# A retention and conformer trunk on one core: the conv module in one written order, scores a head ahead, heads turned amid pooled rows

## The chip, the cores and the metric

The kernel runs on one core of a Trainium2 chip. The metric is the device time of one execution in microseconds (us), as the median of several runs. TensorE (PE) multiplies 128x128 blocks; VectorE (DVE), ScalarE (ACT) and GpSimd (POOL) work on 128-partition tiles in SBUF and PSUM; SyncE (SP) issues the transfers.

## What is computed

512 tokens of width 1024 pass four pre-normalised residual layers: a mixer, a SwiGLU feed-forward layer (FFN), a convolution module, and a second FFN; then a final norm.

```
# mixer: retention (4 heads of 128) beside a pooling mixer
q, k, v, g, u = split(h @ w_in)
scores = einsum('bhncd,bhnmd->bhncm', qc, kc) * decay_mask
o      = scores @ v + cross-chunk state;  o = groupnorm(o) * ret_norm_g
out    = concat([silu(g) * o, pooled(u)]) @ w_out
# conformer conv
a, gate = split(h @ w_pw1 + b_pw1)
u  = a * sigmoid(gate)
dw = depthwise_conv(u, w_dw, width 31, causal) + b_dw
z  = silu(layernorm(dw) * ln_g + ln_b)          # over channels
out = z @ w_pw2 + b_pw2
```

## The kernel before

**Numbers.** Each f32 operand is split into a high part (fp32r) and a low rest, and a product is three matmuls: high by high, low by high, high by low (`mm3`, L224 to L226). Activations lie with channels on the partitions and 512 tokens along the row, eight tiles of 128 channels. Weights come as 1-MB chunks: a transfer (L167), a cast of the high part on ACT (L195), a subtraction for the low part on DVE (L198). PE runs its instructions in the order in which they stand; so do the other engines. PSUM holds three pairs of banks for products ("mm") and two single banks ("aux").

**The mixer.** q and k of a head are split (`parts`), a head's scores are four blocks of products (`ps_s`) that DVE multiplies by the decay mask into `sT` (L516), and the outputs `ps_o` are products of `sT` and v (L520). Head h's scores stand right ahead of its outputs. The out-projection (`ps_wo`) sums over eight rows of blocks, the four pooled ones first; when it reaches a retention head, that head is turned by four transposes (`ps_t`, L563), scaled and split (`mh`, L252), and used at once.

**The conv module.** The first projection runs in eight chunks `ps_pw j` of 48 products with 512 columns; `gated` turns a chunk into u_j (DVE L1085, sigmoid on ACT, DVE L1088). Tiles 0 and 1 are convolved on DVE, 31 multiply-adds each ("taps", L1114). Tiles 2 to 7 are convolved on PE (`ps_c`, L1122): 32 matmuls on 32-row quadrants, of shifted copies R_j of u_j (four transfers inside SBUF, L1103) by diagonal blocks dg_j that POOL multiplies (L1097; two buffers, so dg_j waits for conv tile j-2). The layer norm's sums are taken about a pivot: the mean over channels of tiles 2 and 3, added on DVE (`pivot`, L1183), summed over partitions by PE (`ps_ms`, L304), scaled (L1185), spread to all partitions by PE (`ps_mu`, L312). From then on DVE keeps sums of d and of its square.

For j below 6 the code is a loop, and the instructions of each engine are ordered by a scheduler. From chunk 6 on the order is written out by hand: chunks 6 and 7 and the conv tiles 6 and 7 go in two halves A and B of 256 tokens, and for each half come the sums, `stats`, then `centre`, `swish` (L1167, L1171, L1173) and `split_z` (high part on DVE, L1177; rest, L1178), and the second projection `ps_p` (L245 to L248).

Of the kernel before, what the change touches and what calls it, by code (L numbers as in the profile page):

```python
# [9 lines left out]
F32 = mybir.dt.float32  # L10
# [6 lines left out]
P = 128  # L17
D = 1024
S = 512
# [63 lines left out]
def trunk(ctx: ExitStack, tc: tile.TileContext, a: dict):  # L83
# [54 lines left out]
    halved = {("w_pw1", 6), ("w_pw1", 7), ("w_pw2", 0), ("w_pw2", 1)}  # L138
# [4 lines left out]
    def start_load():  # L143
# [18 lines left out]
        elif i == 1:  # L162
            raw = raws[1]
            for s in CUT[1][1:]:
                nc.sync.dma_start(raw[:, s], a[name][j][:, s])
        else:
            nc.sync.dma_start(raw[:, :kt * c], a[name][j])  # L167
# [69 lines left out]
    def high_first(ps, wh, wl, xh, xl, cols, ks):  # L237

        for low in range(2):
            for k in ks:  # L240
                for i in range(2):
                    c = slice(i * P, (i + 1) * P)
                    o = ps[:, i, cols]
                    if low:
                        nc.tensor.matmul(o, lhsT=wh[:, k, c], rhs=xl[k][:, cols], start=False, stop=k == KT - 1)  # L245
                    else:
                        nc.tensor.matmul(o, lhsT=wh[:, k, c], rhs=xh[k][:, cols], start=k == 0, stop=False)
                        nc.tensor.matmul(o, lhsT=wl[:, k, c], rhs=xh[k][:, cols], start=False, stop=False)  # L248
# [102 lines left out]
    def mixer():  # L351
        nonlocal xin
        with ExitStack() as m:
# [128 lines left out]
            v = [xp.tile([P, S], F32, tag=f"xgl{t}", name=f"v{t}") for t in range(NT)]  # L482
            token_major("v", lambda t, ps: nc.vector.tensor_scalar_mul(v[t], ps, rtok[:, t:t + 1]))


            def parts(h):
                odd = h % 2
                out = []
                for i, src in enumerate((qk[h], qk[4 + h])):
                    if odd:  # L490
# [6 lines left out]
                    out.append((h_, l_))  # L497
                return out


            pos_ = [pair(f"ps_o{i}") for i in range(2)]
            ahead = parts(0)
            for h in range(H):
                (qh, ql), (kh, kl) = ahead
                ahead = parts(h + 1) if h + 1 < H else None
                sT = []
                for j in range(NT):
# [9 lines left out]
                    sT.append(s)  # L517
                for i in range(NT):
# [33 lines left out]
            acc = new_acc()  # L552
            for j2 in range(2):
                ws = [chunk("w_o", 2 * j2 + jj) for jj in range(2)]
                pss = [pair(f"ps_wo{2 * j2 + jj}") for jj in range(2)]
                for ks in ((4, 5, 6, 7), (0, 1, 2, 3)):
                    for jj in range(2):
                        wh, wl = ws[jj]
                        for k in ks:
                            if mh[k] is None:  # L560
                                pt = paux.tile([P, S], F32, tag="aux", name=f"ps_t{k}")
                                for t in range(NT):
                                    nc.tensor.transpose(pt[:, t * P:(t + 1) * P], ret[t][:, k * P:(k + 1) * P], ident)  # L563
                                mh[k] = mx.tile([P, S], F32R, tag=f"xgh{k}", name=f"mh{k}")
                                ml[k] = mx.tile([P, S], F32R, tag=f"xgl{k}", name=f"ml{k}")
                                split_scaled(mh[k], ml[k], pt, V("ret_g", k))
# [496 lines left out]
    def conv(acc):  # L1063
        with ExitStack() as m:
# [10 lines left out]
            us, Rs, dgs = {}, {}, {}  # L1075

            def gated(j, ps, cols, between=lambda: None):
# [12 lines left out]
                if j < NDVE:  # L1090
                    return

                if j not in Rs:
                    Rs[j] = cw.tile([P, 4, 28 + S], F32, tag="R", name=f"R{j}")
# [11 lines left out]
            def conv_tile(j, cols, between={}):  # L1106
                if j < NDVE:
                    o = d[:, j, cols]
                    for q in range(CW):
                        at = slice(1 + q + cols.start, 1 + q + cols.stop)  # L1110
                        if q == 0:
                            nc.vector.tensor_scalar(o, us[j][:, at], V("dwc", CW * j), V("b_dw", j), ALU.mult, ALU.add)
                        else:
                            nc.vector.scalar_tensor_tensor(o, us[j][:, at], V("dwc", CW * j + q), o, ALU.mult, ALU.add)  # L1114
                else:
                    ps = paux.tile([P, S], F32, tag="aux", name=f"ps_c{j}")
                    n = cols.stop - cols.start
                    for g in range(8):
                        if g in between:
                            between[g]()  # L1120
                        for i in range(4):
                            nc.tensor.matmul(ps[32 * i:32 * i + 32, :n], lhsT=dgs[j][:, i, g, :],  # L1122
                                             rhs=Rs[j][:, i, 4 * g + cols.start:4 * g + cols.stop],
                                             start=g == 0, stop=g == 7, skip_group_check=True)
                    return ps[:, :n]
# [11 lines left out]
            def second_sums(j, cols):  # L1137
                sq = s2 if j == PV[0] else wk.tile([P, cols.stop - cols.start], F32, tag="sq", name="sqc")
                nc.scalar.activation(sq, d[:, j, cols], AF.Square)
                if j != PV[0]:  # L1140
                    nc.vector.tensor_tensor(s2[:, cols], s2[:, cols], sq, ALU.add)

            def pivot_tile(j, ps, cols):
# [4 lines left out]
                second_sums(j, cols)  # L1148
# [26 lines left out]
            def split_z(j, cols):  # L1175
                dj = d[:, j:j + 2, cols]
                nc.vector.tensor_copy(zh[:, j:j + 2, cols], dj)  # L1177
                nc.vector.tensor_tensor(zl[:, j:j + 2, cols], dj, zh[:, j:j + 2, cols].bitcast(F32), ALU.subtract)  # L1178
# [3 lines left out]
            def pivot():  # L1182
                nc.vector.tensor_tensor(dsum, d[:, PV[0], :], d[:, PV[1], :], ALU.add)  # L1183
                v = sm.tile([P, NT], F32, tag="lp", name="piv", bufs=1)
                nc.vector.tensor_scalar_mul(v, token_sums(dsum), 1.0 / (2 * P))  # L1185
                row["piv"] = v

            def into_sums(j):
# [4 lines left out]
                second_sums(j, FULL)  # L1193

            pss = []
            for j in range(KT - 2):
                late = {}
                if j == 1:
                    r = inv_rms(acc)
                    late = {5: lambda: row.update(rb=spread(r, "rms"))}  # L1200
                pss.append(pair(f"ps_pw{j}"))
                feature_major(pss[j], *chunk("w_pw1", j), xgh, xgl, between=late)
                if j:
                    rb = row["rb"]
                    for i in (0, 1) if j == 1 else (j,):
                        gated(i, pss[i], FULL)
                if j == PV[1] + 2:
                    pivot()
                if j > NDVE:
                    ps = conv_tile(j - 1, FULL)  # L1210
                if j == PV[1] + 2:
                    spread(row["piv"], "mu", piv)
                    nc.vector.scalar_tensor_tensor(s1, piv, -2.0, dsum, ALU.mult, ALU.add)
                    for i in PV:
                        into_sums(i)
                if j > NDVE:
                    if j - 1 in PV:
                        bias_tile(j - 1, ps)
# [173 lines left out]
```

## Time and profile before

| quantity | value |
|---|---|
| three runs: median, lowest, highest | 1063.51, 1063.12, 1063.87 us |
| profiled execution: time of the run, span of the trace | 1063.56, 1061.8 us |
| mean granted clock of TensorE | 0.997 of full speed |
| busy: PE, weight loads, DVE, ACT, POOL | 1048.1, 913.8, 848.3, 478.3, 19.1 us |
| conv module in the span | about 520 to 700 us |

The span is the time from the first to the last recorded work; 1.76 us of the execution lie around it. Busy times are sums over one engine, and engines overlap. A granted clock of 1.00 is TensorE's 2.4 GHz level, 0.50 its 1.2 GHz level; a stretch that holds both shows a value between.

### The profile page before, as it was taken

What the parts mean: (1) busy time and instruction counts of PE and PEld (TensorE: products, weight loads), DVE (VectorE), ACT (ScalarE), POOL (GpSimd) and SP (SyncE); (2) the same over time, 40 slices, a digit from 0 to 9 for tenths busy, and PEclk for the clock granted to TensorE, in tenths of its full rate; (3) what the DMA queues carried; (4) which work ended last, traced back from release to release, by engine and by line L of the source; (5) the groups of instructions that cost most, each with busy time, mean ns of one, the idle gap of its engine ahead of it and who ended that gap; (6) DMA issues with size and microseconds to landing.
All of it is one profiled execution on the core that took longest, in us unless ns stands there. A gap on an engine that the chain in (4) does not pass through costs nothing.

```text
span 1061.8 us, 16541 instructions
## 1 busy us (share of the span) xinstructions
PE 1048.1 (99%) x6794; PEld 913.8 (86%) x6794; DVE 848.3 (80%) x1270; ACT 478.3 (45%) x820; POOL 19.1 (2%) x10
## 2 busy tenths in 40 slices
PE   9999999999999999999999999999999999999997
PEld 6887878889999999998887567988899999999987
DVE  7977736879988888996769966878799888889855
ACT  7643124555554545543522023455455554455434
POOL 0000000000000000000100310000000000000000
PEclk9999999999999999999999999999999999999999
DMA  8422022422333332334127464142233323233122
GB/s 281 144 80 83 37 80 81 147 94 92 116 108 103 116 104 81 115 119 140 59 80 123 83 124 97 66 149 80 94 115 119 120 84 111 94 110 119 41 80 80
DMA packets 33979, 110.14 MB, mean 104 GB/s; under 512 B 3824, under 2 KB 12016, under 8 KB 25200
## 3 DMA queue, kind: packets, MB, share of 16 engines
q1 hardware_dynamic: 33904, 109.09, 33.2%
q8 instruction: 53, 0.87, 0.4%
q14 instruction: 22, 0.18, 0.1%
HBM read 100.34 MB, written 2.10 MB: 96 GB/s over the span
## 4 chain that ended last, share of the span: by engine, by line
PE 91%; DVE 4%; ACT 2%; issue 2%; DMA 1%; SPq 0%; DVEq 0%; ACTq 0%
PE ps_x L744 19%; PE ps_y L744 9%; PE ps_dn L226 7%; PE ps_dn L225 7%; PE ps_dn L224 7%; PE ps_z L744 5%; PE ps_gu L224 3%; PE ps_gu L226 3%; PE ps_gu L225 3%; PE ps_c L1122 2%; PE ps_pw L224 2%; PE ps_pw L225 2%; PE ps_pw L226 2%; DVE d L1114 2%; PE ps_wo L225 1%
## 5 line engine op out<-in xcount | busy, mean ns | idle before, releaser
L195 ACT CAST w<-wr 128x2048 fp32r<-128x2048 f32 (+4 forms) x49 | 67.0, 1379 | 97.2 <-issue 25.1
L744 PE MATMUL ps_x<-th,w 128*128 128x256 f32 x576 | 109.8, 276 | 0.0
L655 DVE TENSOR_TENSOR wg<-wg 128x512 f32<-128x512 f32 x144 | 99.7, 692 | 4.9
L664 ACT CAST w<-wg 128x512 fp32r<-128x512 f32 x144 | 78.6, 617 | 35.9 <-PE ps_y L744 33.3
L669 DVE TENSOR_TENSOR w<-wg,w 128x2048 fp32r<-128x2048 f32 x36 | 82.5, 2290 | 13.0 <-ACT w L664 13.0
L744 PEld LDWEIGHTS ps_x<-th,w 128*128 128x128 f32 x576 | 92.1, 188 | 0.1
L198 DVE TENSOR_TENSOR w<-wr,w 128x2048 fp32r<-128x2048 f32 (+4 forms) x49 | 79.7, 1636 | 10.4 <-ACT w L195 10.2
L744 PE MATMUL ps_x<-tl,w 128*128 128x256 f32 x288 | 79.5, 276 | 0.0
L334 DVE TENSOR_TENSOR X<-X,ps_dn 128x1024 f32<-128x1024 f32 x46 | 56.0, 1218 | 18.7 <-PE ps_dn L226 18.6
L225 PE MATMUL ps_dn<-hl,dh0d 128*128 128x512 f32 x152 | 59.4, 391 | 0.0
L224 PE MATMUL ps_dn<-hh,dh0d 128*128 128x512 f32 x152 | 59.4, 391 | 0.0
L226 PE MATMUL ps_dn<-hh,dl0d 128*128 128x512 f32 x152 | 59.2, 390 | 0.1
L224 PE MATMUL ps_pw<-xgh,w 128*128 128x512 f32 (+1 forms) x160 | 56.7, 354 | 0.0
L225 PE MATMUL ps_dn<-hl,dh1d 128*128 128x512 f32 x144 | 56.2, 391 | 0.0
L224 PE MATMUL ps_dn<-hh,dh1d 128*128 128x512 f32 x144 | 56.2, 390 | 0.0
L226 PE MATMUL ps_dn<-hh,dl1d 128*128 128x512 f32 x144 | 56.0, 389 | 0.0
L225 PE MATMUL ps_pw<-xgl,w 128*128 128x512 f32 (+1 forms) x160 | 56.0, 350 | 0.0
L226 PE MATMUL ps_pw<-xgh,w 128*128 128x512 f32 (+1 forms) x160 | 55.8, 349 | 0.0
L744 PE MATMUL ps_x<-xgh,w 128*128 128x256 f32 x288 | 55.2, 277 | 0.0
L744 PE MATMUL ps_y<-th,w 128*128 128x256 f32 x288 | 54.8, 276 | 0.0
L744 PE MATMUL ps_y<-xgh,w 128*128 128x256 f32 x288 | 54.8, 276 | 0.0
L744 PEld LDWEIGHTS ps_x<-tl,w 128*128 128x128 f32 x288 | 54.1, 188 | 0.0
(321 smaller groups left out, 2958.4 us busy)
## 6 DMA issues: line engine op xcount, KB each, us to landing
wg<-in_w_gu SPq DMA_DIRECT2D x36, 1024.0 KB, 5.0
dr<-in_w_dn SPq DMA_DIRECT2D x64, 256.0 KB, 2.9
wr<-in_w_pw SPq DMA_DIRECT2D x12, 1024.0 KB, 5.0
wr<-in_w_gu SPq DMA_DIRECT2D x8, 1024.0 KB, 4.9
dr<-in_w_dn SPq DMA_DIRECT2D x32, 192.0 KB, 2.5
R<-u SPq DMA_DIRECT2D x16, 270.0 KB, 8.2
wr<-in_w_o SPq DMA_DIRECT2D x4, 1024.0 KB, 4.9
X<-in_xT SPq DMA_DIRECT2D x8, 256.0 KB, 4.3
```

The lines of the kernel that those rows point to most:

```text
L195: nc.scalar.copy(wh[:, s], raw[:, s])
L198: nc.vector.tensor_tensor(wl[:, s], raw[:, s], wh[:, s].bitcast(F32), ALU.subtract)
L224: nc.tensor.matmul(out, lhsT=wh, rhs=xh, start=start, stop=False)
L225: nc.tensor.matmul(out, lhsT=wh, rhs=xl, start=False, stop=False)
L226: nc.tensor.matmul(out, lhsT=wl, rhs=xh, start=False, stop=stop)
L334: nc.vector.tensor_tensor(xx, xx, ps, sign)
L655: nc.vector.tensor_tensor(o, o, i, ALU.add)
L664: nc.scalar.copy(block(sums[f][0], *SUMS[i]), block(raw_g[f], *SUMS[i]))
L669: nc.vector.tensor_tensor(l, raw_g[f], h.bitcast(F32), ALU.subtract)
L744: nc.tensor.matmul(out, lhsT=u[:, k, :], rhs=v, start=first and k == 0 and n == 0, stop=k == 3 and n == 2, skip_group_check=True)
L1114: nc.vector.scalar_tensor_tensor(o, us[j][:, at], V("dwc", CW * j + q), o, ALU.mult, ALU.add)
L1122: nc.tensor.matmul(ps[32 * i:32 * i + 32, :n], lhsT=dgs[j][:, i, g, :], rhs=Rs[j][:, i, 4 * g + cols.start:4 * g + cols.stop], start=g == ...
```

## The change

Three things are done.

1. **Scores ahead.** In the mixer, `parts(0)`, `scores(0)` and `parts(1)` stand ahead of the v projection. In the loop over heads, `parts(h + 2)` and `scores(h + 1)` stand ahead of the outputs of head h.
2. **Turns.** Heads 0 to 3 are turned at fixed places of the out-projection: heads 0 and 1 ahead of pooled rows 6 and 7 of the second block, heads 2 and 3 ahead of retention rows 0 and 1 of the first.
3. **Conv.** The whole module stands in one written order for PE, DVE, ACT and SP. The taps are handed out in portions, tile 0's first, then tile 1's. Chunks 6 and 7 are whole. The pivot's addition has its own place (`pivot_sum`), at contraction 4 of chunk 6, and the spread at contraction 7. Conv tiles 2 to 4 stand later by one chunk or more; 5, 6A, 7A, 6B and 7B run in a row. R_4 and R_5 lie in the storage of zh and zl (`late`). The eight transfers of R_7 are issued back to back. The high part of z is copied on ACT (`z_hi`), and a small Silu on a tile of its own (`warm`) stands ahead of the pivot tiles. The first two chunks of the second projection hold 4 contractions by 512 columns instead of 8 by 256, each in two transfers of 512 KB, and `out_proj` goes over both pairs of banks for every two contractions.

```diff
-            plan += [("w_pw2", i, 8, 256) for i in range(4)]
+            plan += [("w_pw2", i, 4, 512) for i in range(2)] + [("w_pw2", i, 8, 256) for i in (2, 3)]
...
+            parts(0)
+            scores(0)
+            parts(1)
...
             for h in range(H):
+                sT = scored.pop(0)
+                if h + 2 < H:
+                    parts(h + 2)
+                if h + 1 < H:
+                    scores(h + 1)
...
+            turns = {(1, 6): (0,), (1, 7): (1,), (0, 0): (2,), (0, 1): (3,)}
                         for k in ks:
-                            if mh[k] is None:
...
+                            for n in turns.pop((jj, k), ()):
+                                turned(n)
...
-            def split_z(j, cols):
-                nc.vector.tensor_copy(zh[:, j:j + 2, cols], dj)
+            def z_hi(j, cols):
+                nc.scalar.copy(zh[:, j:j + 2, cols], d[:, j:j + 2, cols])
...
+            def out_proj(w, j, cols):
+                for i, q in enumerate((q0, q1)):
+                    c = slice(2 * P * i, 2 * P * (i + 1))
+                    high_first(q, w[0][:, :, c], w[1][:, :, c], zhs, zls, cols, range(j, j + 2), j // 4 * 4)
...
+                c3 = conv_tile(3, FULL)
+                some_taps(1)
+                gated(5, pss[5], FULL, one_tap)
+                split_lo(hi)
+                to_rows(5, FULL)
+                bias_tile(3, c3)
+                proj(6, {4: lambda: (pivot_sum(), some_taps(1), pivot_mean(), some_taps(4)),
+                         7: lambda: spread(row["piv"], "mu", piv)})
...
+                c4 = conv_tile(4, FULL)
+                gated(6, pss[6], FULL, one_tap)
+                to_rows(6, FULL)
+                proj(7)
...
+                c5 = conv_tile(5, FULL)
+                gated(7, pss[7], FULL)
+                for cols in HALVES:
+                    to_rows(7, cols)
+                nc.scalar.activation(warm, warm, AF.Silu)
+                c6 = conv_tile(6, A, ps=p6[:, 0, :])
+                pivot_tile(5, c5, FULL)
+                c7 = conv_tile(7, A, ps=p7[:, 0, :])
...
+                c7 = conv_tile(7, B, ps=p7[:, 1, :], between={2: lambda: spread(row["A"][1], "lrs", lrs[:, A])})
+                swish(0, A)
+                z_hi(0, A)
+                centre(2, A)
...
+                out_proj(w0, 0, A)
+                out_proj(w0, 2, A)
+                note("B", stats, B)
+                out_proj(w1, 4, A)
+                spread(row["B"][0], "mu", mus[:, B])
+                spread(row["B"][1], "lrs", lrs[:, B])
+                out_proj(w1, 6, A)
+                centre(0, B)
```

What this does to the engines is seen at three places; the lines of the changed kernel are shifted (L1230 is a tap, L1205 the pivot's addition, L1137 a conv product). First DVE around the pivot's addition, in the conv module, before: `d` are the taps, `acc` takes the sum of tiles 2 and 3, `gu` and u5 belong to `gated(5)`, `piv` is the mean.

```order
L1114 SCALAR_TENSOR_TENSOR d_4960<-u1_5110,vec_79,d_4960 128x512
L1114 SCALAR_TENSOR_TENSOR d_4960<-u0_5103,vec_79,d_4960 128x512
L1114 SCALAR_TENSOR_TENSOR d_4960<-u1_5110,vec_79,d_4960 128x512 x4
L1183 TENSOR_TENSOR acc_4963<-d_4960 128x512
L1114 SCALAR_TENSOR_TENSOR d_4960<-u1_5110,vec_79,d_4960 128x512 x3
L1085 TENSOR_TENSOR gu_5445<-ps_pw5_5389,bc_rms_5083 128x1024
L1185 TENSOR_SCALAR piv_5458<-ps_ms_5459 128x4
L1088 SCALAR_TENSOR_TENSOR u5_5443<-gu_5445,vec_79,act_5446 128x512
L198 TENSOR_TENSOR w25_5594<-wr25_5592,w25_5594 128x2048
```

And in the changed kernel:

```order
L1230 SCALAR_TENSOR_TENSOR d_4960<-u1_5175,vec_79,d_4960 128x512 x13
L1103 MEMSET u5_5502 128x31
L1106 TENSOR_TENSOR gu_5504<-ps_pw5_5404,bc_rms_5068 128x1024
L1230 SCALAR_TENSOR_TENSOR d_4960<-u1_5175,vec_79,d_4960 128x512
L1109 SCALAR_TENSOR_TENSOR u5_5502<-gu_5504,vec_79,act_5505 128x512
L204 TENSOR_TENSOR w25_5466<-wr25_5340,w25_5466 128x2048
L1205 TENSOR_TENSOR acc_4963<-d_4960 128x512
L1230 SCALAR_TENSOR_TENSOR d_4960<-u1_5175,vec_79,d_4960 128x512
L1210 TENSOR_SCALAR piv_5553<-ps_ms_5547 128x4
L1230 SCALAR_TENSOR_TENSOR d_4960<-u1_5175,vec_79,d_4960 128x512 x4
```

The addition stood behind the taps that had become ready first; now thirteen taps, the whole of `gated(5)` and the low part of a chunk stand ahead of it, and the taps read one tile's u only.

Next PE at the end of the conv module, before, where `ps_pw7` is the last product of chunk 7's half B, and `ps_p20` the first of the second projection:

```order
L225 MATMUL ps_pw7_5591<-xgl7_4942,w25_5594 128x256
L226 MATMUL ps_pw7_5591<-xgh7_4941,w25_5594 128x256
L1122 MATMUL ps_c6_5989<-R6_5654,dg6_5655 32x256 x8
L312 MATMUL ps_lrs_5998<-con_80,rs_y_5936 128x128 x2
L1122 MATMUL ps_c6_5989<-R6_5654,dg6_5655 32x256 x24
L247 MATMUL ps_p20_6051<-zh_4962,w26_5853 128x256
```

And in the changed kernel, from conv tile 5 on:

```order
L1137 MATMUL ps_c5_5716<-zl_4961,dg5_5514 32x512 x32
L1137 MATMUL ps_c6_5771<-R6_5641,dg6_5642 32x256 x32
L1137 MATMUL ps_c7_5772<-R7_5756,dg7_5757 32x256 x32
L1137 MATMUL ps_c6_5771<-R6_5641,dg6_5642 32x256 x12
L310 MATMUL ps_ms_5864<-con_80,acc_4963 128x1 x2
L310 MATMUL ps_ms_5867<-con_80,s2_4966 128x1 x2
L1137 MATMUL ps_c6_5771<-R6_5641,dg6_5642 32x256 x16
L318 MATMUL ps_mu_5907<-con_80,mean_5870 128x128 x2
L1137 MATMUL ps_c6_5771<-R6_5641,dg6_5642 32x256 x4
L1137 MATMUL ps_c7_5772<-R7_5756,dg7_5757 32x256 x8
L318 MATMUL ps_lrs_5924<-con_80,rs_y_5877 128x128 x2
L1137 MATMUL ps_c7_5772<-R7_5756,dg7_5757 32x256 x24
L253 MATMUL ps_p20_5983<-zh_4962,w26_5589 128x256
```

Chunk 7 is done ahead of these rows, and 5, 6A, 7A, 6B and 7B follow each other; the spread of the inverse deviation stands 24 quarter products ahead of the second projection, and half B of tile 7 no longer stands behind the first products of the second projection.

Last the SP queue, before, where R6 and R7 are the shifted copies, and `wr` raw weights:

```order
L1103 DMA R6_5654<-u6_5647 32x4x284 x4
L167 DMA wr27_5742<-in_w_pw2 128x2048
L1103 DMA R7_5756<-u7_5749 32x4x284 x4
L1103 DMA R6_5654<-u6_5647 32x4x256 x4
L1103 DMA R7_5756<-u7_5749 32x4x256 x4
L167 DMA wr28_6349<-in_w_pw2 128x2048
```

And in the changed kernel, where R_4 lies in zh and R_5 in zl:

```order
L170 DMA wr26_5395<-in_w_pw2 128x4x256 x2
L1127 DMA zh_4962<-u4_5386 32x4x540 x4
L170 DMA wr27_5511<-in_w_pw2 128x4x256 x2
L1127 DMA zl_4961<-u5_5502 32x4x540 x4
L1127 DMA R6_5641<-u6_5633 32x4x540 x4
L173 DMA wr28_5649<-in_w_pw2 128x2048
L1127 DMA R7_5756<-u7_5749 32x4x284 x4
L1127 DMA R7_5756<-u7_5749 32x4x256 x4
L173 DMA wr29_6345<-in_w_pw2 128x2048
```

The two halves of R7 stand behind each other, R6 is one set of whole rows, and the first two chunks of `w_pw2` are two issues each.

## Rows read from the trace of the kernel before

**Rows 1.** The page: the span, and the busy time of each engine with its share of the span and its instructions.
```profile
span 1061.8 us, 16541 instructions
PE 1048.1 (99%) x6794; PEld 913.8 (86%) x6794; DVE 848.3 (80%) x1270; ACT 478.3 (45%) x820; POOL 19.1 (2%) x10
```

**Rows 2.** The waits of TensorE over the whole span: line, what it waited for, microseconds in total, times, longest.
```profile
PE ps_ms L304 <- DVE acc L1183: 1.8, 1, 1.8
PE ps_c L1122 <- DMA R<-u: 1.1, 1, 1.1
PE ps_s L224 <- DVE sT L516: 0.9, 1, 0.9
PE ps_p L247 <- DVE zh L1177: 0.6, 1, 0.6
PE ps_wo L224 <- ACT mh L252: 0.3, 1, 0.3
```

**Rows 3.** The timeline of TensorE around the pivot sum: start, duration, engine, line, operation, tile written and tiles read, stationary shape, moving shape, count; in brackets the idle time before it and its releaser.
```profile
604.67 0.39 PE L224 MATMUL ps_pw<-xgh,w 128*128 128x512 f32 x1
605.12 0.39 PE L226 MATMUL ps_pw<-xgh,w 128*128 128x512 f32 x1
607.27 1.05 PE L304 MATMUL ps_ms<-con,acc 128*128 128x1 f32 x8 [1.76 <-DVE acc L1183]
...
608.73 0.38 PE L225 MATMUL ps_pw<-xgl,w 128*128 128x256 f32 x1
...
612.11 0.31 PE L226 MATMUL ps_pw<-xgh,w 128*128 128x256 f32 x1
```

**Rows 4.** The stretch from 608 to 613 us: its length, then busy time and instructions of PE, of the weight loads, of DVE, ACT and POOL, then the granted clock, the DMA share and GB/s.
```profile
608.00:613.00 5.00, 5.00 (x32) 4.51 (x36) 3.37 (x5) 2.32 (x2) 0.00 (x0) 0.66 0.00 0
```

**Rows 5.** The timelines of DVE and of POOL, the taps of two conv tiles (L1114), the multiplies that make the diagonals (L1097) and the pivot's addition (L1183), in order of time; columns as in rows 3.
```profile
585.73 3.40 DVE L1114 SCALAR_TENSOR_TENSOR d<-u,vec,d 128x512 f32<-128x512 f32 x5
588.94 7.92 POOL L1097 TENSOR_TENSOR dg<-vec,con 128x1024 f32<-128x1024 f32 x1 [59.78 <-PE ps_c L1122]
...
602.06 2.42 POOL L1097 TENSOR_TENSOR dg<-vec,con 128x1024 f32<-128x1024 f32 x1 [5.20 <-PE ps_c L1122]
602.75 2.29 DVE L1114 SCALAR_TENSOR_TENSOR d<-u,vec,d 128x512 f32<-128x512 f32 x1
605.07 0.75 DVE L1114 SCALAR_TENSOR_TENSOR d<-u,vec,d 128x512 f32<-128x512 f32 x1
605.86 0.75 DVE L1114 SCALAR_TENSOR_TENSOR d<-u,vec,d 128x512 f32<-128x512 f32 x1
606.53 0.68 DVE L1183 TENSOR_TENSOR acc<-d 128x512 f32<-128x512 f32 x1
...
630.78 1.92 POOL L1097 TENSOR_TENSOR dg<-vec,con 128x1024 f32<-128x1024 f32 x1 [9.27 <-PE ps_c L1122]
```

**Rows 6.** The timeline of TensorE in the mixer, at the scores of head 0.
```profile
100.79 0.34 PE L226 MATMUL ps_s<-q,kyl 128*128 128x384 f32 x1
102.02 0.39 PE L224 MATMUL ps_s<-q,kyh 128*128 128x256 f32 x1 [0.90 <-DVE sT L516]
```

**Rows 7.** The timeline of TensorE at the end of the conv, products of the second projection (L245) and second half of conv tile 7 (L1122).
```profile
661.82 0.63 PE L245 MATMUL ps_p<-zl,w 128*128 128x256 f32 x4
663.59 3.66 PE L1122 MATMUL ps_c<-R,dg 128*32 128x256 f32 x64 [1.14 <-DMA R<-u]
```

**Rows 8.** Two long runs of conv products: one piece of the chain that ended last (start, length, engine, tile, line, count), and a stretch with columns as in rows 4.
```profile
612.42 7.00 PE ps_c L1122 x64
595.00:601.80 6.80, 6.80 (x64) 1.82 (x56) 6.80 (x10) 0.00 (x0) 1.86 (x1) 1.00 0.99 210
```

**Rows 9.** The timelines of ACT and DVE from the spread of the inverse deviation to the first half of z; and from the page the FFN's casts of 128x512 on ACT (busy in all, mean ns of one).
```profile
657.47 0.37 ACT L316 COPY lrs<-ps_lrs 128x256 f32<-128x256 f32 x1
657.87 1.28 ACT L1173 ACT_TABLE_LOAD   x1
659.16 2.08 ACT L1173 ACTIVATE d<-d,vec 128x256 f32<-128x256 f32 x4
659.09 0.68 DVE L1171 TENSOR_TENSOR d<-d,lrs 128x512 f32<-128x512 f32 x1
660.29 0.43 DVE L1177 CAST zh<-d 128x512 fp32r<-128x512 f32 x1 [0.51 <-ACT d L1173]
...
L664 ACT CAST w<-wg 128x512 fp32r<-128x512 f32 x144 | 78.6, 617 | 35.9 <-PE ps_y L744 33.3
```

**Rows 10.** The transfers that fill a conv tile's R: the issues of the first half of tile 7 on the SP queue, how long after issue they landed, and the piece of the chain in which the second half is under way.
```profile
630.41 2.50 SPq L1103 DMA_DIRECT2D R<-u  x4
DMA to landing us min/median/max: 3.1/3.8/4.2
659.86 3.59 DMA R<-u
```

**Rows 11.** Groups by line and shape in the conv, 520 to 700 us: count, busy time, mean ns of one, idle time ahead and releasers.
```profile
L198 DVE TENSOR_TENSOR w<-wr,w 128x2048 fp32r<-128x2048 f32 x8 | 18.3, 2293 | 2.7 <-ACT w L195 2.6
L1085 DVE TENSOR_TENSOR gu<-ps_pw,bc_rms 128x1024 f32<-128x1024 f32 x6 | 7.3, 1225 | 4.8 <-ACT bc_rms L316 4.1 <-PE ps_pw L226 0.7
L1088 DVE SCALAR_TENSOR_TENSOR u<-gu,vec,act 128x512 f32<-128x512 f32 x6 | 4.5, 750 | 1.6 <-ACT act L1086 1.6
L1135 ACT ACTIVATE d<-ps_c,vec 128x512 f32<-128x512 f32 x2 | 1.4, 688 | 18.5 <-PE ps_c L1122 18.5
```

More of the change, by code (lines that the diff above doesn't have):

```diff
@@ L496, in parts, with scores @@
                     split(h_, l_, src)
[L497 to L505, printed above, removed]
+                    qkp[h] += [h_, l_]
+            def scores(h):
+                qh, ql, kh, kl = qkp.pop(h)
                 sT = []
@@ L1192, in into_sums, with some_taps @@
                     nc.vector.tensor_tensor(s1, s1, dj, ALU.add)
[L1193 to L1218, printed above, removed]
-                    else:
-                        pivot_tile(j - 1, ps, FULL)
-            for j in range(NDVE):
-                conv_tile(j, FULL)
-                into_sums(j)
+                rest = second_sums(j, FULL)
+                between()
+                rest()
+            taps = iter([(j, q) for j in range(NDVE) for q in range(CW)])
+            def some_taps(n):
+                for j, q in itertools.islice(taps, n):
+                    o, src = d[:, j, :], us[j][:, 1 + q:1 + q + S]
+                    if q == 0:
+                        nc.vector.tensor_scalar(o, src, V("dwc", CW * j), V("b_dw", j), ALU.mult, ALU.add)
+                    else:
+                        nc.vector.scalar_tensor_tensor(o, src, V("dwc", CW * j + q), o, ALU.mult, ALU.add)
             A, B = HALVES
@@ L1229, in note, with split_next, split_hi, split_lo @@
                 row[name] = f(*args)
+            def split_next(pieces=1):
+                for _ in split_load(pieces):
+                    pass
+            def split_hi():
+                load = split_load(1, True)
+                next(load)
+                return load
+            def split_lo(load):
+                for _ in load:
+                    pass
+                start_load()
+            def one_tap():
+                some_taps(1)
+            def proj(j, between={}):
+                pss[j] = pair(f"ps_pw{j}")
+                feature_major(pss[j], *chunk("w_pw1", j, 0), xgh, xgl, between=between)
@@ L1253, in conv @@
+                c6 = conv_tile(6, B, ps=p6[:, 1, :], between={3: lambda: note("A", stats, A), 7: lambda: spread(row["A"][0], "mu", mus[:, A])})
                 centre(0, A)
[L1254 to L1256 removed]
+                c7 = conv_tile(7, B, ps=p7[:, 1, :], between={2: lambda: spread(row["A"][1], "lrs", lrs[:, A])})
                 swish(0, A)
+                z_hi(0, A)
@@ L1264, in conv @@
-                pivot_tile(6, c6, B)
+                rest()
                 swish(6, A)
-                split_z(4, A)
+                z_hi(6, A)
                 w0 = chunk("w_pw2", 0, 0)
+                w1 = chunk("w_pw2", 1, 0)
                 q0, q1 = [pair(f"ps_p2{j}") for j in range(2)]
-                high_first(q0, *w0, zhs, zls, A, range(2))
-                pivot_tile(7, conv_tile(7, B), B)
-                split_z(6, A)
-                for _ in range(3):
-                    next(load)
@@ L1274, in conv @@
-                feature_major(q0, *w0, zhs, zls, A, {5: lambda: note("B", stats, B)}, ks=range(2, KT))
-                w1 = chunk("w_pw2", 1, 0)
-                feature_major(q1, *w1, zhs, zls, A, {0: lambda: spread(row["B"][0], "mu", mus[:, B]),
-                                                     3: lambda: spread(row["B"][1], "lrs", lrs[:, B]),
-                                                     4: lambda: (centre(0, B), next(load))})
+                out_proj(w0, 0, A)
+                out_proj(w0, 2, A)
```

215 lines of the change are left out of this document (133 added, 82 removed).

## The prediction

> **What bounds the kernel now.** I read the busy times first: PE is busy for 1048.1 of 1061.8 us [rows 1], and the next busiest, the weight loads beside it and DVE, have 86% and 80%. So only two things can shorten the kernel: PE idle time, and PE products that run below full rate. The waits of TensorE come next, since they say where its 13.7 us of idle time can be had [rows 2]: five named waits in the stages that the change touches, 4.7 us by the view's own count. A wait's count leaves out the pipeline's restart, so I went to the timeline of each and measured from the start of the last product before to the start of the next one, less the usual spacing.
>
> - Pivot sum. From 604.67 to 605.12 two products of 512 columns start, 0.225 apart. The next product starts at 607.27, 2.15 after 605.12 [rows 3]: 1.92 lost. Behind it the granted clock is 0.66 over five microseconds [rows 4], between the 2.4 GHz and 1.2 GHz levels: PE had stood still for about 2 us before it. The 16 spacings of 256-column products from 608.73 to 612.11 take 3.38 [rows 3]. At half of the 512-column spacing, 0.113, they would take 1.81: 1.57 lost.
> - Scores of head 0: 100.79 to 102.02 is 1.23 [rows 6]; a product of 384 columns takes 3/4 of 0.225, 0.17. 1.06 lost.
> - Conv tile 7, second half: four products start at 661.82, so the next could start at 662.27 (4 x 0.113); it starts at 663.59 [rows 7]. 1.32 lost.
> - First product of the second projection: 0.6, and the first product on a turned head: 0.3 [rows 2].
>
> Together 1.92 + 1.57 + 1.06 + 1.32 + 0.60 + 0.30 = 6.77 us. That is all that these stages can give on PE.
>
> **What the change removes.** The products are the same in number of columns: chunks 6 and 7 go from two products of 256 to one of 512, 0.225 either way. So I take each loss in turn.
>
> *Pivot sum (3.49).* Before, the addition stands in DVE's order behind taps, one of which took 2.29 at 602.75 instead of 0.75, while POOL's multiply of 602.06 ran; it starts at 606.53 [rows 5], when PE is already waiting. Now PE asks for it 24 products of chunk 6 after conv tile 3 has ended: 24 x 0.225 = 5.4 us. From that end ACT needs 0.69 for the bias [rows 11] and DVE 0.68 for the addition [rows 5], some 1.45 with the passing of semaphores. That leaves 4.0 us in which DVE may be late. Is it? Taps of one tile that follow each other start 0.79 apart (605.07, 605.86), where taps alternating between two tiles took 0.66 each (five in 3.40 with the last one's tail, at 585.73) [rows 5]: 62 x 0.13 = 8 us more on DVE in all. In chunks 2 to 4 DVE has 1.23 + 2.29 + 0.75 [rows 11] and ten taps of 0.79, 12.2 us, for PE's 48 x 0.225 = 10.8: it falls back 1.4 a chunk, 4.2 in three. Then PE has conv tile 2, chunk 5 and conv tile 3 ahead, 7.0 + 10.8 + 7.0 = 24.8 us [rows 8], while DVE has two gatings and low parts (8.5) and 16 taps (12.6), 21.1: 3.7 of the 4.2 is made good before the addition is due, and 0.5 against 4.0 is left. POOL's multiplies hold a tap by 1.5 each (2.29 for 0.75) in both kernels. I take the whole 3.49 as removed, with 0 as the other end. Without the 4.0 us of cover it would all come back.
>
> *Scores (1.06) and turned heads (0.3).* The masked blocks `sT` of head 0 now have the v projection between them and their use, those of later heads a head's outputs. A turned head now has twelve products of 512 columns between its transposes and its use, 2.7 us, where it had none and waited 0.3. New are small waits where the scores of a head want an aux bank that DVE has not yet read. No row shows that order; I take 0.3, with 0 and 1.06 (the present wait, kept) as ends.
>
> *R7 (1.32).* Before, its second half was issued only behind the second half of `gated(7)`, and was under way for 3.59 us to the end of the wait [rows 10]. Now both halves go out after chunk 7. The chain for the first half is 1.23 + 0.69 (sigmoid, as long as the bias over 512 columns [rows 11]) + 0.75 + 6.15 (first issue 630.41, four issues 0.6 apart, last landing at most 4.2 after the last [rows 10]) = 8.8 us; PE has conv tile 5 and tile 6 A meanwhile, 7.0 + 3.66 = 10.7 [rows 7, 8]. 1.9 us of slack. The second half comes behind it by 2.5 us of issuing, when PE has 7.3 more. Removed, with 1.32 as the other end.
>
> *First product on z (0.60).* Before, the inverse deviation was copied at 657.47, ACT then loaded its table for 1.28, and two Silus and DVE's cast followed until 660.72 [rows 9]. The table load is now made earlier, behind `gated(7)`. The chain left is copy 0.37, DVE multiply 0.68, two Silus 1.04 (four in 2.08), and ACT's copy of the high part, which no row has in this place; the FFN's casts of that shape on ACT take 0.617 [rows 9]. That is 2.71, and about 0.4 for four hand-overs: 3.1. PE's cover is the last 24 of 32 steps of tile 7 B, 24/32 x 3.66 = 2.75 us [rows 7]. So a wait of about 0.4 stands there (ends 0 and 1.0). The copy on ACT costs DVE nothing and ACT 8 x 0.62 = 5 us, where it is 45% busy [rows 1].
>
> **What it adds.** Half B has no such neighbour as before: its mean and deviation are spread ahead of the last 24 products of half A, 24 x 0.113 = 2.7 us. Behind them stand a copy 0.37, centre 0.68 and multiply 0.68 on DVE, Silu 1.04, copy 0.62 = 3.4. I take a wait of 0.7, with ends 0.3 and 1.5 (four hand-overs, and a DVE that is still in half A). The waits at 102.02 and 663.59, 1.06 and 1.32, show products at normal spacing behind them [rows 6, 7], so I charge no clock for these. The transfers of `w_pw2` in four pieces are issued three chunks ahead, and cost nothing unless they hold the queue ahead of R7.
>
> **The sum.** -6.77 + 0.4 + 0.7 + 0.3 = -5.4 us. Against the profiled run, 1063.56 (span 1061.8 and 1.76 around it; 0.05 above the median): **1058.2 us**. With the ends of the three new waits (0.3 to 3.6 in all) 1057.1 to 1060.4; 0.7 lower if the scheduled order of the loop held small losses on PE that no wait in the rows names: 1056.4 to 1060.4 for this case.
>
> **The rivals.**
>
> *Diagonals of tile 7 late.* dg_7 has the buffer of dg_5, so POOL may start only when conv tile 5 has ended, and PE wants it 3.66 us later, after tile 6 A. POOL's multiply took 1.92 at 630.78, when DVE ran few taps, and 7.92 at 588.94, beside taps in a row [rows 5]. Nearest is 1.92: all taps stand ahead of tile 5 in the new order. With 7.92 the wait is 4.3, and the clock falls as at 608, 1.6 more: 1064.1, no change. The Trainium skill's page "SBUF — State Buffer", section "Who interferes with whom", says that a DVE instruction with two SBUF inputs and a GpSimd instruction that reads SBUF lock each other out, each for one whole instruction: by it POOL would wait at most for one low part of 2.29, a wait of 0.55 and 1058.8 us; the row of 7.92 doesn't agree, since it is 6.0 longer than the shortest.
>
> *The pivot wait stays.* If DVE is over 4.0 us late at the addition, for instance because taps held by POOL cost more than 1.5 each, 3.49 comes back: 1061.7, no change. Speaking for it: the taps' 8 us; against: the 24.8 to 21.1.
>
> *The clock falls in the conv run (the slower side).* Tiles 5, 6 and 7 now run 7.0 + 4 x 3.66 = 21.6 us of conv products without any other. These are products on 32-row quadrants. The longest such run in the rows is 7.0 at 1.00 [rows 8], and nothing longer is shown. If the chip lowers the clock there to the 1.2 GHz level, each microsecond of run costs another: the whole would be +21.6, 1079.8; from 7.4 us of it the kernel is slower by over 0.2%. For it speaks only that no run of this length is shown.
>
> *New waits larger.* If the waits at the two halves grow past 2 us each, as the one at 605 did, each takes the clock with it: 2 x (2.0 + 1.6) in place of 1.1, 1064.3.
>
> **How the numbers follow.** Likeliest as above 0.68; diagonals late 0.09; pivot wait stays 0.09; clock 0.08; larger waits 0.06. 0.2% is 2.1 us, about what a measurement tells from no change: faster is below 1061.4, slower above 1065.6. Faster: 0.67 of the likeliest, and a part of the mixed cases (a smaller delay of the diagonals, of the pivot or of a half) 0.09, 0.76. Slower: the clock 0.07 and both mishaps at a half 0.02, 0.09. Same: 0.15. The range for 8 in 10 runs from 1056.4 to 1062.2, where the pivot's case is taken in and the diagonals' worst is left out.
>
> **What will show it.** Right: no wait at the pivot sum and granted clock 1.00 behind it; no wait for R in conv tile 7; 1.00 through the 21.6 us run; waits of about 0.4 and 0.7 ahead of the first z products of each half. The pivot step is wrong if `ps_ms` still waits for DVE. The forecast is wrong if a wait of over 2 us shows anywhere in the conv module, or if the granted clock drops in it.

## The result and the profile after

The changed kernel takes 1057.1 us at the median (1056.76 to 1057.6), the kernel before 1063.69 in the runs taken with it: a ratio of 0.9935, with a 95% interval of 0.9918 to 0.9952. That is 6.6 us less, where 5.4 were forecast. The profiled execution took 1056.82 us. First the page of the changed kernel, the span and the engines, against [rows 1]:

```profile
span 1055.0 us, 16333 instructions
PE 1045.5 (99%) x6698; PEld 909.3 (86%) x6698; DVE 849.7 (81%) x1257; ACT 483.4 (46%) x826; POOL 16.3 (2%) x10
```

PE has 96 products fewer, since chunks 6 and 7 are whole, and it is busy for 2.6 us less, while the span is 6.8 shorter: 4.2 us of the gain are idle time, and most of the rest are products that ran slow before (1.57 of it at the low clock, by the prediction's reading of [rows 3]). The waits of TensorE, as in [rows 2] (line, what it waited for, total, times, longest):

```profile
PE ps_idle L122 <- DVE zero L119: 1.2, 1, 1.2
PE ps_p L253 <- ACT zh L1196: 0.8, 2, 0.5
PE ps_qk L230 <- DVE qk L421: 0.3, 1, 0.3
PE ps_qk L231 <- DVE xgl L259: 0.2, 1, 0.2
```

Four of the five waits of [rows 2] are gone. The fifth, at the first product on z, is now a wait for ACT's copy in place of DVE's cast, and stands in both halves. The other three lie in the first 42 us of the mixer and stood there before. At the pivot sum, DVE's addition, POOL's multiply beside it and PE's products (timelines, as in [rows 3, 5]); POOL's multiply for conv tile 7; the first products on z of halves A and B; and two stretches with columns as in [rows 4]:

```profile
603.92 2.16 DVE L1205 TENSOR_TENSOR acc<-d 128x512 f32<-128x512 f32 x1 [0.17 <-ACT d L1150]
603.31 2.22 POOL L1121 TENSOR_TENSOR dg<-vec,con 128x1024 f32<-128x1024 f32 x1 [14.51 <-PE ps_c L1137]
608.41 0.39 PE L232 MATMUL ps_pw<-xgh,w 128*128 128x512 f32 x1
608.64 0.95 PE L310 MATMUL ps_ms<-con,acc 128*128 128x1 f32 x8
641.41 2.24 POOL L1121 TENSOR_TENSOR dg<-vec,con 128x1024 f32<-128x1024 f32 x1 [14.82 <-PE ps_c L1137]
657.96 0.39 PE L253 MATMUL ps_p<-zh,w 128*128 128x256 f32 x1 [0.24 <-ACT zh L1196]
671.67 0.39 PE L253 MATMUL ps_p<-zh,w 128*128 128x256 f32 x1 [0.53 <-ACT zh L1196]
608.00:613.00 5.00, 5.00 (x28) 4.24 (x27) 3.08 (x5) 0.00 (x0) 0.00 (x0) 1.00 1.07 205
634.00:657.30 23.30, 23.30 (x334) 12.00 (x336) 14.64 (x32) 7.30 (x12) 2.24 (x1) 1.00 0.50 117
```

The addition waits 0.17 us for ACT's bias, so DVE is not late. It takes 2.16 us instead of 0.68: POOL's multiply runs beside it until 605.53. It ends at 606.08; PE asks 2.56 later and goes on without a gap. The granted clock is 1.00 where it was 0.66, and 1.00 through the 23.3 us of conv products and the few sums and spreads among them.

Where the time went is read from where stages begin. Each line is the first product of a stage in the timeline of PE: the FFN behind the mixer, the conv module, and the FFN behind it, in the kernel before and after.

```profile
185.63 0.39 PE L224 MATMUL ps_gu<-xgh,w 128*128 128x512 f32 x1
518.64 0.45 PE L224 MATMUL ps_pw<-xgh,w 128*128 128x512 f32 x1
711.39 0.39 PE L224 MATMUL ps_gu<-xgh,w 128*128 128x512 f32 x1
...
183.52 0.39 PE L230 MATMUL ps_gu<-xgh,w 128*128 128x512 f32 x1
516.54 0.44 PE L230 MATMUL ps_pw<-xgh,w 128*128 128x512 f32 x1
704.51 0.39 PE L230 MATMUL ps_gu<-xgh,w 128*128 128x512 f32 x1
```

The mixer has become 2.1 us shorter, the first FFN between is the same (333.01 and 333.02), and the conv module has gone from 192.75 to 187.97, 4.8 us shorter. That is 6.9 us by these two traces, where the medians give 6.6.

### The profile page after: what moved, and what is told of

It reads as the page before. It is cut to its first block, busy times and chain, and to the rows that moved or that the text cites. A ratio compares the mean times of both kernels' runs of the same rounds, so it can differ in the third digit from the quotient of the medians.

```text
span 1055.0 us, 16333 instructions
## 1 busy us (share of the span) xinstructions
PE 1045.5 (99%) x6698; PEld 909.3 (86%) x6698; DVE 849.7 (81%) x1257; ACT 483.4 (46%) x826; POOL 16.3 (2%) x10
## 4 chain that ended last, share of the span: by engine, by line
PE 95%; ACT 2%; DVE 2%; DMA 0%; issue 0%; SPq 0%; DVEq 0%; ACTq 0%
PE ps_x L764 19%; PE ps_y L764 9%; PE ps_dn L232 7%; PE ps_dn L231 7%; PE ps_dn L230 7%; PE ps_z L764 5%; PE ps_c L1137 4%; PE ps_pw L230 3%; PE ps_gu L230 3%; PE ps_pw L232 3%; PE ps_pw L231 3%; PE ps_gu L232 3%; PE ps_gu L231 3%; PE ps_wo L232 1%; PE ps_wo L231 1%; PE ps_wo L230 1%
## 5 line engine op out<-in xcount | busy, mean ns | idle before, releaser
L845 ACT COPY sn<-ps_x 128x256 f32<-128x256 f32 x36 | 13.5, 374 | 84.4 <-PE ps_x L764 84.4
L788 DVE TENSOR_TENSOR hl<-act,hh 128x512 fp32r<-128x512 f32 x44 | 30.4, 691 | 26.6 <-ACT hh L787 26.6
L230 PE MATMUL ps_pw<-xgh,w 128*128 128x512 f32 x128 | 50.6, 396 | 0.0
```

Source lines behind the costliest of these rows:

```text
L230: nc.tensor.matmul(out, lhsT=wh, rhs=xh, start=start, stop=False)
L788: return lambda: nc.vector.tensor_tensor(hl[f], s, hh[f].bitcast(F32), ALU.subtract)
```

## The experiments

**The two parts apart.** The mixer's part was put into the kernel before, and the mixer of before into the changed kernel.

```diff
# mixer_alone: the kernel before, with
+            parts(0); scores(0); parts(1)
...
+                if h + 2 < H:
+                    parts(h + 2)
+                if h + 1 < H:
+                    scores(h + 1)
...
+            turns = {(1, 6): (0,), (1, 7): (1,), (0, 0): (2,), (0, 1): (3,)}
# conv_alone: the changed kernel without these
```

> The kernel before with the mixer's part of the change alone (scores a head ahead, turns amid pooled rows). By the prediction's terms it gives 1.06 + 0.3 - 0.3 = 1.1 us: 1062.6 against 1063.7. By what the two traces show of spacing lost on TensorE up to 230 us (5.9 before, 4.3 after) 1.6 us: 1062.1. If all of the gain were the conv module's, no change: 1063.7.

> The changed kernel with the mixer of before. By the prediction's terms 3.49 + 1.32 + 0.6 - 0.4 - 0.7 = 4.3 us under the kernel before: 1059.4. By what the two traces show of spacing lost in the conv module (46.8 before, 41.7 after, the usual steps of conv products included) 5.0 us: 1058.7. With the mixer's part alone the two gains should add up to the whole, 6.6; if the mixer's order also shifts the conv module's transfers, they don't.

Measured: the mixer alone 1061.43 (ratio 0.9974, 0.9964 to 0.9984) and the conv module alone 1059.16 (0.9955, 0.9938 to 0.9971), both against 1063.79. That is 2.4 and 4.6 us, together 7.0 against 6.6 of the whole: within the intervals, each about a microsecond to either side or more, the parts add up. The traces say the same more closely: with the mixer's part alone the FFN behind it starts at 183.53, with the conv part alone the conv module takes 188.23. The conv module's gain is the forecast one within 0.3. The mixer's is twice what was forecast.

**Which part of the mixer.** The turns alone, in the kernel before:

```diff
-                            if mh[k] is None:
-                                (transposes and split of head k)
...
+                            for n in turns.pop((jj, k), ()):
+                                turned(n)
```

> The kernel before with the turns alone. The prediction took 0.3 us for it, the wait of the view: 1063.4. By the sums of spacings in the traces of before and of the mixer's part alone, transposes (2.17 to 1.42) and out-projection (44.37 to 43.99), it is 1.1 us: 1062.5. The scores a head ahead are then the rest of the mixer's gain.

Measured: 1062.45 against 1063.49, ratio 0.9992 (0.9982 to 1.0001). The medians differ by the 1.0 us that was expected, but the interval holds no change as well, so the timeline decides. First the start of the FFN behind the mixer with the turns alone, then the kernel before where a turned head is first used:

```profile
184.53 0.39 PE L224 MATMUL ps_gu<-xgh,w 128*128 128x512 f32 x1
...
149.98 1.04 PE L563 MATMUL ps_t<-con,ret 128*128 128x128 f32 x8
151.35 0.73 PE L224 MATMUL ps_wo<-mh,w 128*128 128x512 f32 x2 [0.34 <-ACT mh L252]
152.14 0.50 PE L225 MATMUL ps_wo<-ml,w 128*128 128x512 f32 x1
152.47 0.40 PE L226 MATMUL ps_wo<-mh,w 128*128 128x512 f32 x1
```

184.53 against 185.63 is 1.10 us for the turns, which leaves 1.0 (to 183.52) for the scores and what little else shifted. Counted from the start of the v projection (76.25 before, 76.24 with the turns, 76.14 after) the three stretches are 109.38, 108.29 and 107.38, and the other traces with the changed mixer have 107.33 to 107.39: the split is clear of the scatter. The eight transposes are those of two heads, so a turn of two heads stands in one piece ahead of its use. The rows show why 0.34 was too small a price. From 151.35 to 152.47 three products start, where 0.225 each would make 0.68: 0.45 more are lost behind the wait, as the low part `ml` is late too and the next product follows at a wider spacing (152.14 to 152.47, 0.33 for 0.225). The remaining 0.3 of the 1.10 are not in these rows. The list of waits has the 0.34 alone.

**The cover of the pivot sum.** Taps were moved ahead of the addition, from behind it.

```diff
-    proj(6, {4: lambda: (pivot_sum(), ...
+    proj(6, {4: lambda: (some_taps(3), pivot_sum(), ...     # sum_behind_3; 8 in sum_behind_8
```

> The changed kernel with three more taps ahead of the pivot's addition on DVE, taken from behind it. In the trace after, the addition ends at 606.08 and TensorE asks for it at 608.64, a cover of 2.56 us. Three taps of 0.79 are 2.4 us: if the cover is what hides the addition, no wait at the pivot sum and 1057.1 us. If the addition were on the path already, 2.4 us more: 1059.5.

> The same with eight taps ahead of the addition, 6.3 us. By the cover of 2.56 a wait of 3.8 us at the pivot sum, and by the drop of the granted clock seen behind the wait of before some 1.6 us more: 1062.5. Without a drop of the clock 1060.9. If DVE's lateness did not matter, 1057.1.

Measured: 1057.13 with three taps, no wait; 1063.73 with eight (0.9995, 0.9986 to 1.0005, against 1063.79). The timeline of DVE with three; then those of PE and DVE with eight, and three stretches of five microseconds, the first of which holds the wait:

```profile
603.74 3.98 DVE L1230 SCALAR_TENSOR_TENSOR d<-u,vec,d 128x512 f32<-128x512 f32 x3
607.64 0.69 DVE L1205 TENSOR_TENSOR acc<-d 128x512 f32<-128x512 f32 x1
...
608.96 0.39 PE L232 MATMUL ps_pw<-xgh,w 128*128 128x512 f32 x1
612.81 1.87 PE L310 MATMUL ps_ms<-con,acc 128*128 128x1 f32 x8 [3.46 <-DVE acc L1205]
612.07 0.68 DVE L1205 TENSOR_TENSOR acc<-d 128x512 f32<-128x512 f32 x1
608.00:613.00 5.00, 1.54 (x7) 0.96 (x7) 4.82 (x8) 0.00 (x0) 0.00 (x0) 0.88 1.06 192
613.00:618.00 5.00, 5.00 (x16) 4.32 (x17) 0.58 (x2) 0.00 (x0) 0.00 (x0) 0.50 0.75 106
618.00:623.00 5.00, 5.00 (x25) 3.93 (x24) 0.60 (x1) 0.59 (x1) 0.00 (x0) 0.93 0.00 0
```

With three, a tap stands beside POOL's multiply in the addition's place: the three take 3.98, the addition 0.69. It ends at 608.33, 0.4 ahead of PE. With eight, the stop from 608.96 to 612.81 costs 3.85 - 0.23 = 3.6 us, near the 3.8 expected. The clock then stands at 1.2 GHz through 613 to 618, half rate, which costs 2.5 us there, and some 0.4 in all around it: 6.5 in this trace, against 6.6 by the medians. The low clock cost more than the 1.6 that was expected from the wait of before, and it is not the same each time: the ten executions took 1062.1 to 1064.54, four of them 1063.03 or less at a mean granted clock of 0.997, the others 0.995 or 0.996. So the first three taps cost nothing and the next five cost more than their own length: running out of 2.56 us of cover at this one place costs as much as the whole change gains.

**Taps in turn.** Tiles 0 and 1 in turn, as before the change:

```diff
-            taps = iter([(j, q) for j in range(NDVE) for q in range(CW)])
+            taps = iter([(0, q) for q in range(9)] + [(j, q + 9 * (1 - j)) for q in range(22) for j in range(NDVE)] + ...)
```

> The changed kernel with the taps of tiles 0 and 1 in turn, from the tenth on. Taps should start 0.66 apart instead of 0.79, some 5 us less on DVE. By the prediction DVE is off the path in the conv module, so the time stays at 1057.1 and the cover at the pivot sum, 2.56 us, does not shrink. If DVE's longer row of taps costs anything now, the time falls.

Measured: 1057.11, and the waits of the changed kernel unchanged. In DVE's and POOL's timelines, the taps beside a multiply of POOL, and the pivot's addition:

```profile
584.28 10.36 DVE L1231 SCALAR_TENSOR_TENSOR d<-u,vec,d 128x512 f32<-128x512 f32 x13
585.40 2.06 POOL L1121 TENSOR_TENSOR dg<-vec,con 128x1024 f32<-128x1024 f32 x1 [58.20 <-PE ps_c L1137]
604.12 1.85 DVE L1205 TENSOR_TENSOR acc<-d 128x512 f32<-128x512 f32 x1 [2.20 <-ACT d L1150]
```

DVE is busy for 846.3 us instead of 849.7, 3.4 less where some 5 were expected, and its longer row of taps costs nothing. DVE is 2.2 us early at the addition, but the cover grows by 0.3 alone (it ends at 605.97, and PE asks at 608.84), since the addition waits for ACT's bias and not for taps.

The multiply of 585.40 bears on the 7.92 us of [rows 5]. In the kernel before, the taps beside that multiply and the first break in their row are these:

```profile
585.07 12.35 DVE L1114 SCALAR_TENSOR_TENSOR d<-u,vec,d 128x512 f32<-128x512 f32 x16
595.05 0.08 DVE L1082 MEMSET u<- 128x31 f32 x1
```

The multiply ends at 596.86, 1.8 us behind the start of the memset, and undisturbed it takes 1.92, so it looks as if it had stood still until then. But here a multiply beside thirteen taps in turn took 2.06, so such a row does not hold POOL up by itself.

**The diagonals of tile 7.** Five taps and the sums of tile 1 were kept back until POOL multiplies.

```diff
-                some_taps(12)
+                some_taps(8)
...
-                some_taps(NDVE * CW)
                 into_sums(0)
-                into_sums(1)
...
                 split_next()
+                some_taps(NDVE * CW)
+                into_sums(1)
```

> The changed kernel with five taps and the sums of tile 1 kept back until POOL multiplies the diagonals of tile 7. In the trace after POOL needs 2.24 us for them beside other work, from 641.41, and TensorE wants them at 644.7. If each DVE instruction with two inputs from SBUF holds POOL back at most once, 3 us and no wait at conv tile 7. If POOL stays locked out while taps follow each other, as 7.92 us of the trace before suggests, 4.0 + 1.9 = 5.9 us, a wait of 2.6 there and a fall of the clock. Either way DVE is later at half A's sums by 6 us, of which 2 are idle now: up to 4 us of wait at ps_ms and 1.6 by the clock, up to 1062.7.

Measured: 1064.57, above the 1062.7 that was the highest expected. The wait that has come, the timelines of POOL and DVE, and the stretches from 645 on:

```profile
PE ps_c L1137 <- DVE d L1165: 3.7, 1, 3.7
641.31 2.23 POOL L1121 TENSOR_TENSOR dg<-vec,con 128x1024 f32<-128x1024 f32 x1 [14.82 <-PE ps_c L1137]
641.69 5.55 DVE L1230 SCALAR_TENSOR_TENSOR d<-u,vec,d 128x512 f32<-128x512 f32 x5
645.00:650.00 5.00, 3.27 (x63) 2.04 (x52) 4.83 (x7) 0.63 (x1) 0.00 (x0) 1.00 0.56 196
650.00:655.00 5.00, 3.02 (x26) 1.30 (x26) 3.95 (x9) 1.46 (x3) 0.00 (x0) 0.58 0.02 3
655.00:660.00 5.00, 5.00 (x40) 2.84 (x39) 2.34 (x15) 0.00 (x0) 0.00 (x0) 0.50 0.00 0
660.00:665.00 5.00, 5.00 (x68) 3.19 (x68) 1.93 (x4) 1.25 (x4) 0.00 (x0) 0.89 0.01 3
```

POOL needs 2.23 us beside five taps, which take 5.55 instead of 3.9 (four spacings of 0.79 and the last one's 0.75): POOL is not locked out, it holds one tap. The wait came elsewhere than either theory had it: tile 6 B starts only when DVE has read tile 6 A (L1165), and DVE was late with it. Both halves are written into one PSUM tile of two banks, which is the likely reason; no run takes them apart. The wait did reach the size expected for DVE's lateness, 3.7, and in this trace the clock stayed low for longer behind it than at the pivot.

**The table load and ACT's copy.** Without the early Silu, and with the high part of z on DVE, right behind its Silu or one group later:

```diff
-                nc.scalar.activation(warm, warm, AF.Silu)                     # late_table
-                nc.scalar.copy(zh[:, j:j + 2, cols], d[:, j:j + 2, cols])
+                nc.vector.tensor_copy(zh[:, j:j + 2, cols], d[:, j:j + 2, cols])   # zhi_dve
-                z_hi(0, A)                                                    # zhi_dve_later:
                 swish(2, A)
+                z_hi(0, A)                                                    # each one group later
```

> The changed kernel without the early Silu on a tile of its own, so that ACT loads its table when the first Silu of half A comes. In the trace after, the first product on z waits 0.24 us, 0.61 from the start of the product before. By the chain of the prediction the load of 1.28 us stands in it: a wait of 1.5, and 1058.4 against 1057.1. If the load is made while ACT waits for DVE's multiply (0.76 us of idle time there), only 0.5 more: 1057.6.

> The changed kernel with the high part of z made on DVE, as before (0.43 us each instead of 0.62 on ACT). If only the chains' lengths count, 0.2 us less at each half's first product: 1056.7. If DVE is the fuller engine between 655 and 667 us (no idle time over 0.1 there in the trace after), four casts of 0.43 stand ahead of half B's sums and push its spreads back by up to 1.7 us, of which 0.4 is free: a wait of some 1.8 at half B, 1058.2.

> The changed kernel with the high part of z on DVE, each cast one group later in DVE's order, behind the next group's multiply, as before the change; right behind its own Silu it made DVE stand still for 1.16 us each time, and the time 1067.3. If the standing still was the price, and not the cast's place on DVE, most of those 10 us go: the first product of each half then waits for the next group's multiply, 0.9 us more than now, and four casts of 0.43 push half B's sums back by up to 1.7, of which 0.4 is free: 1058 to 1060. If DVE is simply too full for the casts, it stays near 1067.

Measured: 1057.55, 1067.32 (ratio 1.0033, 1.002 to 1.0046) and 1057.78. The load alone is 1.28 us, but it begins with DVE's multiply (655.58 to 656.27), for which ACT would have waited anyway, and the Silus follow it at 656.86 (first two rows below), so 0.5 is left: the second reading held. The cast on DVE cost 10 us, far outside both expectations; behind these two rows, the largest wait and DVE's timeline with the cast in the copy's place:

```profile
655.56 1.28 ACT L1193 ACT_TABLE_LOAD   x1
656.86 1.09 ACT L1193 ACTIVATE d<-d,vec 128x256 f32<-128x256 f32 x2
...
PE ps_p L251 <- DVE zl L1199: 6.3, 3, 3.0
657.31 0.43 DVE L1196 CAST zh<-d 128x512 fp32r<-128x512 f32 x1 [1.16 <-ACT d L1193]
660.95 0.43 DVE L1196 CAST zh<-d 128x512 fp32r<-128x512 f32 x1 [1.16 <-ACT d L1193]
664.81 0.43 DVE L1196 CAST zh<-d 128x512 fp32r<-128x512 f32 x1 [1.16 <-ACT d L1193]
```

DVE stands still for 1.16 us at each cast, behind a Silu that could start only after DVE's own multiply: the two engines take turns, and these groups take 3.6 to 3.9 us each. PE then waits for the low parts, which come behind the casts. This trace is of the shortest of five executions (1065.78, mean granted clock 0.997); the others have 0.993 to 0.996, so a part of the 10 us is the clock's. One group later in the order, with the same casts on the same engine (and, in half B, the low parts a place elsewhere), 9.5 of the 10 us are gone. So the copy on ACT is worth some 0.7 us, and the order of the instructions on DVE is worth the rest.

**A version that takes the two waits away.** The deviation's spread of half A at the start of tile 7 B, and the mean's of half B twelve products earlier:

```diff
-   c7 = conv_tile(7, B, ps=p7[:, 1, :], between={2: lambda: spread(row["A"][1], "lrs", lrs[:, A])})
+   c7 = conv_tile(7, B, ps=p7[:, 1, :], between={0: lambda: spread(row["A"][1], "lrs", lrs[:, A])})
-   out_proj(w1, 4, A)
-   spread(row["B"][0], "mu", mus[:, B])
+   out_proj(w1, 4, A, lambda: spread(row["B"][0], "mu", mus[:, B]))    # between its two pairs of banks
```

> The changed kernel with half A's spread of the inverse deviation at the start of conv tile 7 B instead of a quarter in (8 of its 32 products, 0.9 us), and half B's spread of the mean twelve products earlier (1.4 us), so that its centring is done when the deviation comes. In the trace after, the first products on z wait 0.24 us in A and 0.53 in B (0.61 and 0.81 from start to start, of which 0.31 and 0.11 are usual). If these chains are what ends last there, both waits go and 0.3 + 0.7 = 1.0 us with them: 1056.1. If DVE has no room for half B's centring ahead of its multiply, 0.3 alone: 1056.8.

Measured: 1056.43 (1056.33 to 1056.87), ratio 0.9935 (0.9923 to 0.9948). Its median is 0.7 under that of the changed kernel, where 1.0 was expected, though the intervals against the kernel before cannot tell the two apart. The wait for `zh`, 0.8 in two, is 0.2 in one:

```profile
PE ps_p L253 <- ACT zh L1196: 0.2, 1, 0.2
657.99 0.38 PE L253 MATMUL ps_p<-zh,w 128*128 128x256 f32 x1
668.77 0.69 DVE L1191 TENSOR_TENSOR d<-d,lrs 128x512 f32<-128x512 f32 x1 [0.46 <-ACT lrs L322]
671.30 0.39 PE L253 MATMUL ps_p<-zh,w 128*128 128x256 f32 x1 [0.18 <-ACT zh L1196]
```

In half A no wait is left in the list. In half B the multiply now follows the deviation's copy with the centring done, and what is left is the chain behind it.

## Why the prediction was right, step by step

- **Bound and place.** PE's idle time and slow products were the only things to be had, and they were where the five waits stood. Right: four of the five are gone, and the fifth is down to 0.24 in half A, with 0.53 new in half B, as the forecast had it in kind.
- **Pivot sum.** Right in size: the wait and the low clock are both gone. The cover was put at 4.0 us less a lag of 0.5; the trace has 2.56. The lag was not there, but the addition itself took 2.16 for 0.68 beside POOL's multiply, a price that the text named for taps and left out of this chain; the cover was wide enough to bear it. Three and eight taps show that the cover is what hides the addition. No clock was charged for the waits at 102.02 and 663.59. [rows 6] shows a single product behind the first and so no spacing, but the granted clock of the kernel before is 1.00 from 102 to 107 and from 663.6 to 668.
- **Scores.** Forecast 1.06 - 0.3 = 0.76; the mixer's 2.1 less the turns' 1.1 is 1.0. The 0.3 stood for new waits at the aux banks, and no wait of `ps_s` is in the list after. The order came out otherwise than the text had it: in the trace after the v projection begins at 76.14, as before, and head 0's scores stand amid its second half, from 88.99 to 94.98. Its products from there to 101.69, 6.7 us, and head 1's first scores are what stands between them and the first output at 102.89; that was enough.
- **Turned heads.** The term that was mis-sized: 0.3 was taken from the view of waits, and 1.1 was there. For the other waits I had measured from start to start; for this one and for the first product on z I took the view's count.
- **R7.** Right: no wait for R. Both halves are issued in a row, and tiles 5 and 6 A cover the first.
- **First products on z.** 0.4 and 0.7 were forecast. The view counts 0.24 and 0.53; from start to start, less what is usual at that place (0.31 and 0.11), they cost 0.3 and 0.7. Moving the spreads removed the first and, by the view, 0.35 of the second's 0.53, so they were these chains.
- **Sum.** By the traces, mixer 2.1 for 1.1 forecast, conv 4.8 for 4.3: the missing 1.5 (1.2 by the medians) is 0.8 at the turns, 0.2 at the scores, and 0.5 in the conv module. Of the latter 0.2 is the first product on z, counted from start to start; 0.3 stays open, about as much as the same conv module differs by between traces (187.97 here, 188.23 with the conv part alone).
- **Rivals.** The diagonals of tile 7 took 2.24 us, near the lower bound, and were done at 643.65, 1.1 us before tile 6 A ended. The rule of the Trainium skill's page "SBUF — State Buffer", section "SBUF: two separate sides", that the lock is held for one whole instruction, agrees with this kernel and with the run that put five taps beside POOL (2.23). The 7.92 of the kernel before [rows 5] does not follow from it, and by the run with taps in turn a row of taps does not do it by itself: its cause is open. The clock stayed at 1.00 through the conv run, so the slower side did not come. Nor did the cover at the pivot fail; its 2.56 us were more than the diagonals' 1.1, but it is the rival that a run shows to take the whole gain: with eight taps ahead of the addition the kernel is at the time of before.

## What to carry to other kernels

Price a wait from the start of the last product before it to where the products run at their usual spacing again: the count in the list of waits was 0.34 where 1.1 could be had, and 1.8 where 3.5 could, 1.57 of it at the low clock. When an instruction is moved ahead of a wait, measure how much cover it has and what can eat it, here one low part of 2.3 us, or three taps. When an operation moves to another engine, look at the order it gets there before its duration: 0.43 against 0.62 us said nothing about 10 us.

## What had not been expected of the hardware

- A stop of 3.6 us of PE costs 6.6 at the median: behind 3.46 us of waiting the granted clock stood at 0.50 for 5 us of sums and projection products. Behind 1.76 us it had shown 0.66 over five [rows 4].
- In the trace with five taps beside POOL the clock stayed low for longer behind a wait of about the same length, among conv products: 0.58 and 0.50 over ten microseconds behind 3.7 us, against 0.50 and 0.93. The 23.3 us of conv products without a stop ran at 1.00, so they do not lower the clock themselves. These are one execution each, and no run shows what decides.
- The price changes from one execution to the next. Of the ten with the five taps one took 1061.51 us at a mean granted clock of 0.999, 4.4 over the changed kernel, little more than the wait; another took 1062.69 at 0.997, and the other eight 1064.15 to 1065.54 at 0.994 or 0.995.
